# An output projection moved from feature-major tiles to a token-major group in seven products, with the embedding's projection moved in front of the MLP

## The chip, the cores and the metric

One core of one Trainium2 chip runs the whole program. The metric is the device time of one execution in microseconds (us); lower is better. An execution of the kernel before took 951.73 us in the median of three (951.28 to 951.88).

## What is computed

One layer of a decoder trunk on 512 tokens with 1024 features, all in 32-bit floats:

```python
mix = (sigmoid(gA) * (oA @ w_o_gla) + sigmoid(gB) * (oB @ w_o_attn)) @ w_out
x  += mix
x  += relu(RMSNorm(x) @ w_mlp1)^2 @ w_mlp2      # D_FF = 4096
x  += sigmoid(RMSNorm(x) @ w_pg) * (p @ w_pp)   # p: 512 x 256
out = RMSNorm(x)
```

The change touches the product with `w_out` (1024 x 1024), the residual x behind it, and the product `p @ w_pp` (256 x 1024).

## The kernel before, in words

*Products.* A 32-bit operand is kept as two parts in fp32r, a rounded "hi" and the rest "lo". A product takes three matmuls: hi by hi, hi by lo, lo by hi (`three`). ACT makes hi by a copy, DVE makes lo by a subtraction; this pair is called a split here. Weights come in pieces of 128 x 1024 (512 KB), about 250, through `fetch` (L306 to L325): while one operand is in use, DVE makes the lo of a later one (L297), ACT the hi of the next (L319), and a further one is loaded on SP's queue. All three happen in a fixed order in the engines' instruction streams, each of which is worked off strictly in order.

*Three forms of a projection.* `fm` is feature-major: the weight is the stationary operand, all 512 tokens stream, and a tile of 128 features takes 8 x 3 matmuls of 512 columns. `strassen` and `wide` use the scheme with seven products in place of eight of half the size: the weight quarters A11 to A22 and their sums S1 to S4 meet the activation quarters B11 to B22 and their sums T1 to T4. `strassen` is feature-major with 256 columns a matmul; `wide` is token-major: the activations are stationary, and the weight streams with 512 columns. A stage is one of the seven products: 24 matmuls. Stages share PSUM banks: a bank must be read (`begin`, a copy by ACT into SBUF) before a later stage accumulates into it, and `end` adds a bank to that copy. The order of stages in `wide`:

```python
WIDE = (("A11", "B11", "a"), ("S1", "T1", "c"), ("S2", "T2", "a"), ("A12", "B21", "b"), ("S3", "T3", "a"),
        ("S4", "B22", "c"), ("A22", "T4", "a"))
WBEGIN = {0: ((0, 0), "a"), 1: ((1, 1), "c"), 2: ((0, 1), "a")}
```

*Order of the work.* The program is written out by a generator. PE's stream is the frame; behind every few matmuls (`run`, in pieces) one deferred step of the list `later` is issued on the other engines, and one of the generators in `side`. So what an engine does, and when, follows from where a step was put on the list.

*Around the change.* `og` (the product with `w_o_gla`) makes 8 feature-major tiles; DVE multiplies each by its gate and adds it to the other branch (L1278, L1279), which gives the tiles of `mix`, split by `split_later` or, the last, by `split`. `wo` makes 8 feature-major tiles from them; each is added by DVE to the tile `xx[j]` of the transposed input (L1367, loaded by POOL at L1289). `x1_tile` scales each tile by the norm's weight (L1330) and makes the operands of `m1` (the first MLP projection, 8 groups `m1q0` to `m1q7` in `strassen`) with their sums and splits. During `m1q0`, `to_tokens` transposes the residual on PE (L1310, 32 transposes) and ACT copies it (L1314), since the second MLP projection adds token-major; `stats` sums the squares over the features with four one-column matmuls (L498).

*The embedding.* `pp0` and `pp1` (2 x 4 tiles of 128 tokens, 48 matmuls of 512 columns, `tmaj`) stand between the second MLP projection and `pg`, the last projection, which starts with tokens 0. ACT evacuates them (L1577). They lie beside the transposes (L1488) and splits of x3, the operand of `pg`.

Of the kernel before, what the change touches and what calls it, by code (L numbers as in the profile page):

```python
# [48 lines left out]
def weight_units():  # L49
# [39 lines left out]
    fm("wo", "w_out", 0, 8)  # L89
# [6 lines left out]
    for j in range(2):  # L96
        u.append((f"pp{j}.0", "tm", "w_pp", 0, j * 512))
# [79 lines left out]
NU, NW, PIECE, WAYS = 67, 5, 8, 2  # L177
# [6 lines left out]

NWARM = 9
# [3 lines left out]
def block_kernel(ctx, tc, xT, ws, pT, wts, wha, wa2, vec, lnf, rel, onehot, ident_d, mask_d, out):  # L189
    nc = tc.nc  # L190
    V, S, TE, SY, GP = nc.vector, nc.scalar, nc.tensor, nc.sync, nc.gpsimd

    const = ctx.enter_context(tc.tile_pool(name="const", bufs=1))
# [64 lines left out]
    def sums(i):  # L258
        q, _, what = OPERANDS[i].partition(".")
        if q.startswith("m2c"):  # L260
            if what[:3] == "S2.":
                w = raw[OPERANDS[i]] = raw[f"{q}.S1{what[2:]}"]
                V.tensor_tensor(w, w, raw[f"{q}.A11{what[2:]}"], op=OP.add)
            elif OPERANDS[i] in S4_LOADED:
                w = raw[OPERANDS[i]]
                V.tensor_tensor(w, w, raw[f"{q}.S2{what[2:]}"], op=OP.add)
        elif what[:3] in ("S2.", "S4."):
# [33 lines left out]
    def fetch(upto):  # L301

        while done[0] < min(upto, len(OPERANDS) - 1):
            i = done[0] = done[0] + 1
            if i >= 0:
# [6 lines left out]
                if q.startswith("m2c") and what[:2] == "S2" and f"{q}.S4{what[2:]}" not in S4_LOADED:  # L312
                    w = raw[f"{q}.S4{what[2:]}"] = raw[OPERANDS[i]]
                    GP.dma_start(w, wts[UNIT[f"{q}.A12{what[2:]}"]], accum_op=OP.add)
# [38 lines left out]
    def tmaj(name, n, lhs, evac, tts=range(4)):  # L353
# [3 lines left out]
        for tt in tts:  # L357
# [3 lines left out]
            if tt < 3:  # L361
                run(mms)
# [53 lines left out]
    def wide(name, xo, finish):  # L416


        bank, sums = {}, {}

        def begin(m, t, n, b):
            def go():
                sums[m, t, n] = u32()
# [6 lines left out]
        for i, (op, xname, b) in enumerate(WIDE):  # L430
# [76 lines left out]
    def rms_gen(acc, res, wait=0, gap=0, squared=False):  # L507
# [15 lines left out]
        bc = const.tile([P, T], F32, tag="rstd", name="rstd", bufs=2)  # L523
# [751 lines left out]
    mix = [None] * KC  # L1275
    for j in range(KC):
# [9 lines left out]
    xx = []  # L1286
    for j in range(KC):
        t = u32()
        GP.dma_start(t, xT[j * P:(j + 1) * P, :])  # L1289
        xx.append(t)  # L1290

    acc1, norm2 = [], []
    x2 = {}

    def stats():
        for _ in range(30):
            yield
        r = rms_tok(acc1[0], True)
        n = const.tile([P, 4], F32, name="nrm2")
# [3 lines left out]
    def to_tokens():  # L1303
        for m in range(2):
            for t in range(2):
                pts = [smt() for _ in range(2)]
                for n in range(2):
                    tok = slice((2 * t + n) * P, (2 * t + n + 1) * P)
                    for i in range(4):
                        TE.transpose(pts[n][:, i * P:(i + 1) * P], xx[4 * m + i][:, tok], ident)  # L1310
                yield
                for n in range(2):
                    x2[m, t, n] = u32()
                    S.activation(x2[m, t, n], pts[n], AF.Copy)  # L1314
                yield

    blk, xop = [None, None], {}
    def operand(name, g, x):
        xop[name, g] = split(x)

    def x1_tile(j):

        x, c = xx[j], cv[:, C_LN2 + j:C_LN2 + j + 1]
        g, p, k = j // 4, j % 4 // 2, j % 2

        def first():
            if blk[g] is None:
                blk[g] = [[u32(), u32()], [u32(), u32()]]
            for t in range(2):
                V.tensor_scalar(blk[g][k][t][:, halves(p)], x[:, halves(t)], c, None, op0=OP.mult)  # L1330
            sq = square(x)
            if j:
                V.tensor_tensor(acc1[0], acc1[0], sq, op=OP.add)
            else:
                acc1.append(sq)

        def left():
            (b11, b12), _ = blk[g]
            operand("B11", g, b11)
            t1 = u32()  # L1340
            V.tensor_tensor(t1, b11, b12, op=OP.subtract)
            operand("T1", g, t1)
            blk[g].append(t1)

        names, srcs, his = ("T4", "T2", "B21", "B22", "T3"), [], []

        def sums():
            (_, b12), (b21, b22), t1 = blk[g]
            t2, t3, t4 = u32(), u32(), u32()
            minus(t2, t1, b22)  # L1350
            minus(t4, t2, b21)
            his.append(split_hi(t4))
            V.tensor_tensor(t3, b22, b12, op=OP.subtract)
            srcs.extend((t4, t2, b21, b22, t3))

        def splits(i):
            def go():
                if i < 4:
                    his.append(split_hi(srcs[i + 1]))
                xop[names[i], g] = split_lo(srcs[i], his[i])  # L1360
            return go

        return [first] + {2: [left], 3: [sums] + [splits(i) for i in range(5)]}.get(j % 4, [])

    for j in range(KC):
        ps = fm(f"wo.{j}", mix)
        V.tensor_tensor(xx[j], xx[j], ps, op=OP.add)  # L1367
        later.extend(x1_tile(j))
    side.append(stats())
    side.append(to_tokens())  # L1370


    hid, hb, hx = [None] * 8, {}, {}
# [75 lines left out]
    pt, lnb = [], []  # L1449
# [48 lines left out]
    def last_inputs():  # L1498
        for k in range(2):
# [247 lines left out]
```

## Time and profile before

| | |
|---|---|
| median of three executions | 951.73 us |
| the profiled execution, its own time | 951.71 us |
| span in the profile | 949.6 us |
| PE busy (matmul) | 941.3 us, 99% |
| DVE busy | 726.5 us, 77% |
| ACT busy | 540.8 us, 57% |
| POOL busy | 102.9 us, 11% |
| chain that ended last | PE 98% |
| granted clock, mean | 0.998 |

Busy time is time in which an engine has an instruction at work; neighbours on one engine overlap, so the sum of single durations is longer. The chain is followed back from the last instruction, at each step to what released it. A duration in a row that ends in "x3" is that of three instructions together; where one starts is a better price than how long it lasts, since the next starts before it ends.

### The profile page before, as it was taken

How to read it: one execution, taken by the hardware profiler on the slowest of the kernel's cores; microseconds unless marked ns; L12 is line 12 of the kernel's file. 1: busy time of each engine (PE TensorE's matmuls, PEld its weight loads, DVE VectorE, ACT ScalarE, POOL GpSimd, SP SyncE). 2: the span in 40 equal slices, each digit the busy share in tenths (PEclk: the TensorE clock that was granted, in tenths of full speed). 3: DMA queues.
4: the chain of work that ended last, by engine and by line, in shares of the span. 5: the costliest groups of instructions: out<-in, count | busy, mean ns of one | idle time of the engine just before them, and what ended most of it. 6: DMA issues, size and time to landing. Idle time of an engine off the chain costs nothing.

```text
span 949.6 us, 15089 instructions
## 1 busy us (share of the span) xinstructions
PE 941.3 (99%) x5892; PEld 849.4 (89%) x5892; DVE 726.5 (77%) x1029; ACT 540.8 (57%) x880; POOL 102.9 (11%) x143
## 2 busy tenths in 40 slices
PE   9999999999999999999999999999999999999997
PEld 8789998899988888999988889999999888888886
DVE  7698879866789589878855788677777788988554
ACT  7357546445675479775732448555566445555643
POOL 0150010120100012022020000001000010020000
PEclk9999999999999999999999999999999999999999
DMA  9474482973818466456563436655647546796102
GB/s 352 142 236 114 129 201 68 289 234 100 200 46 227 159 144 182 132 134 200 156 199 92 131 89 173 154 142 134 162 129 191 141 100 166 218 306 222 53 0 89
DMA packets 46022, 150.34 MB, mean 158 GB/s; under 512 B 6723, under 2 KB 7311, under 8 KB 45952
## 3 DMA queue, kind: packets, MB, share of 16 engines
q1 hardware_dynamic: 29664, 100.61, 31.1%
q0 software_dynamic: 12608, 44.26, 23.5%
q10 hardware_dynamic: 3680, 4.51, 1.3%
q8 instruction: 46, 0.75, 0.3%
q14 instruction: 24, 0.20, 0.1%
HBM read 143.03 MB, written 8.17 MB: 159 GB/s over the span
## 4 chain that ended last, share of the span: by engine, by line
PE 98%; issue 1%; DMA 0%; ACT 0%; DVE 0%; POOLq 0%; POOL 0%; DVEq 0%
PE mmt L333 78%; PE smt L333 10%; PE mmt L581 2%; PE smt L1015 2%; PE smt L955 1%; PE smt L878 1%; PE smt L848 0%; PE smt L972 0%; PE smt L961 0%; PE smt L847 0%; PE smt L971 0%; PE smt L1310 0%; PE smt L1171 0%; PE smt L1071 0%; DMA cv<-in_vec_dram 0%
## 5 line engine op out<-in xcount | busy, mean ns | idle before, releaser
L333 PE MATMUL mmt<-ur,hi 128*128 128x256 f32 (+1 forms) x2320 | 476.0, 302 | 0.0
L333 PEld LDWEIGHTS mmt<-ur,hi 128*128 128x128 f32 x2320 | 373.1, 188 | 16.6
L333 PE MATMUL mmt<-ur,lo 128*128 128x256 f32 (+1 forms) x1160 | 351.2, 303 | 0.0
L297 DVE TENSOR_TENSOR lo<-w,hi 128x1024 fp32r<-128x1024 f32 x248 | 302.1, 1221 | 56.9 <-PE mmt L333 35.9
L319 ACT ACTIVATE hi<-w 128x1024 fp32r<-128x1024 f32 x248 | 259.2, 1054 | 93.8 <-PE mmt L333 24.5
L333 PE MATMUL mmt<-hi,ur 128*128 128x512 f32 (+3 forms) x832 | 241.1, 374 | 0.0
L333 PEld LDWEIGHTS mmt<-ur,lo 128*128 128x128 f32 x1160 | 218.6, 188 | 8.2
L333 PEld LDWEIGHTS mmt<-hi,ur 128*128 128x128 f32 x832 | 150.3, 188 | 25.7
L333 PE MATMUL mmt<-lo,ur 128*128 128x512 f32 (+3 forms) x416 | 154.8, 372 | 0.0
L461 ACT ACTIVATE ur<-u 128x512 fp32r<-128x512 f32 x111 | 66.1, 624 | 87.2 <-DVE u L1279 30.9
L333 PEld LDWEIGHTS mmt<-lo,ur 128*128 128x128 f32 x416 | 78.2, 188 | 13.6
L297 DVE TENSOR_TENSOR ur<-u,ur 128x512 fp32r<-128x512 f32 x110 | 72.7, 688 | 11.8 <-ACT ur L461 9.5
L333 PE MATMUL smt<-hi,ur 128*128 128x512 f32 x256 | 79.1, 390 | 0.0
L454 DVE TENSOR_TENSOR u<-u,mmt 128x512 f32<-128x512 f32 (+1 forms) x88 | 54.2, 647 | 26.9 <-PE mmt L333 26.6
L401 ACT ACTIVATE u<-mmt 128x512 f32<-128x512 f32 x72 | 43.1, 598 | 52.6 <-PE mmt L333 52.5
L250 POOL DMA_DIRECT2D w<-in_wts_dram x42 | 40.2, 1001 | 246.1 <-DMA w<-in_wts_dram 94.0
L333 PEld LDWEIGHTS smt<-hi,ur 128*128 128x128 f32 x256 | 47.8, 188 | 9.8
L276 POOL DMA_DIRECT2D w<-in_wts_dram x18 | 16.1, 894 | 317.9 <-DVE w L273 156.9
L333 PE MATMUL smt<-lo,ur 128*128 128x512 f32 x128 | 49.8, 389 | 0.0
L1389 ACT ACTIVATE u<-u 128x512 f32<-128x512 f32 x24 | 15.0, 628 | 26.7 <-DVE u L1385 26.7
L333 PEld LDWEIGHTS smt<-lo,ur 128*128 128x128 f32 x128 | 24.0, 188 | 5.0
L1250 ACT ACTIVATE u<-u 128x256 f32<-128x256 f32 x32 | 11.4, 411 | 20.9 <-DVE u L454 20.9
(235 smaller groups left out, 838.1 us busy)
## 6 DMA issues: line engine op xcount, KB each, us to landing
w<-in_wts_dram SPq DMA_DIRECT2D x180, 512.0 KB, 4.7
w<-in_wts_dram POOLq DMA_DIRECT2D x64, 512.0 KB, 6.8
u<-in_xT_dram SPq DMA_DIRECT2D x8, 256.0 KB, 5.3
u<-in_ws_dram SPq DMA_DIRECT2D x8, 256.0 KB, 5.4
v_dram<-u ACTq DMA_DIRECT2D x8, 256.0 KB, 6.6
u<-v_dram POOLq DMA_DIRECT2D x8, 256.0 KB, 6.2
y_dram<-u ACTq DMA_DIRECT2D x8, 256.0 KB, 2.0
u<-y_dram POOLq DMA_DIRECT2D x8, 256.0 KB, 6.2
```

The costliest lines, as they stand in the source:

```text
L250: GP.dma_start(w, wts[UNIT[b]], accum_op=OP.add)
L276: GP.dma_start(w, wts[UNIT[f"{q}.A21"]], accum_op=OP.add)
L297: V.tensor_tensor(lo, x, hi.bitcast(F32), op=OP.subtract)
L319: S.activation(hi[:, s], w[:, s], AF.Copy, scale=1.0 if c is None else c)
L333: TE.matmul(o, lhsT=l, rhs=r, start=a, stop=b, skip_group_check=shared)
L401: S.activation(sums[c], bank[b], AF.Copy, scale=-scale if c[0] else scale)
L454: V.tensor_tensor(out, s, ps, op=OP.subtract if m else OP.add)
L461: S.activation(hi, x, AF.Copy)
L581: TE.matmul(q0ps[i], lhsT=(hi, hi, lo)[j][:, c], rhs=(xh, xl, xh)[j], start=not k and not j, stop=k == KC - 1 and j == 2)
L1015: TE.matmul(o, lhsT=l[a][:, lc], rhs=r[b], start=start and i == 0, stop=stop and i == 2)
L1250: S.activation(outs[n], s[:, halves(n)], AF.Sigmoid)
L1389: S.activation(s, s, AF.Square)
```

## The change

1. `wo` becomes a token-major group in seven products (`quadw` weights, 14 operands in place of 8 tiles; `wide`). The sums of the weights are made as for the other groups, by DVE (L275 of the changed kernel) or by accumulating loads on POOL (L253, L319).
2. `mix_pair` makes the stationary operands of `wo` during `og`: per pair of tiles two 256-wide subtractions (L1299, L1300), two 256-wide sums (`minus`, L622), splits of both tiles (L474, L302), and for every second pair splits of the sums T1, T2, T4.
3. The residual x is loaded token-major on POOL. `begin` and `end` of `wo` add PSUM banks straight onto it on DVE (L467); a third copy isn't made. As each quarter is finished, `x1_ready` transposes it (L1380, 4 x 8 transposes), ACT copies it scaled (L1388), and sums and splits follow.
4. The sum of squares is taken token-major: eight `Square` with an accumulator on ACT (L1360), then three small DVE operations (L1363 to L1365) whose results scale m1's outputs. The one-column matmuls are gone.
5. `pp0` and `pp1` stand between `wo` and `m1`. ACT evacuates each tile (L1449) and issues its DMA to DRAM (L1450); eight POOL loads (L1588) bring them back during the second MLP projection.
6. `pg` takes tokens in the order 2, 3, 0, 1.

The core of the diff:

```diff
-    fm("wo", "w_out", 0, 8)
+    quadw("wo", "w_out", (0, 512))
+    for j in range(2):
+        u.append((f"pp{j}.0", "tm", "w_pp", 0, j * 512))
...
+TTS = (2, 3, 0, 1)
...
-    def wide(name, xo, finish):
+    def wide(name, xo, finish, base=None):
...
-        bank, sums = {}, {}
+        bank, sums = {}, dict(base or {})
         def begin(m, t, n, b):
             def go():
+                if base:
+                    return add(m, base[m, t, n], base[m, t, n], bank[b][n])
                 sums[m, t, n] = u32()
...
-                later.extend(end(m, t, n, b) for n in range(2))
+                ends = [end(m, t, n, b) for n in range(2)]
+                if base:
+                    later[0:0] = ends
+                else:
+                    later.extend(ends)
...
+    def mix_pair(pr):
+        e, f = tb[2 * pr], tb[2 * pr + 1]
+        g, o = pr // 2, halves(pr % 2)
+        t1, t2, t4 = (msums[name][g][:, o] for name in ("T1", "T2", "T4"))
+        his = {}
+        def sums():
+            V.tensor_tensor(t1, e[:, halves(0)], e[:, halves(1)], op=OP.subtract)
+            V.tensor_tensor(e[:, halves(1)], f[:, halves(1)], e[:, halves(1)], op=OP.subtract)
+            his["e"] = split_hi(e)
+        def second():
+            mix[2 * pr] = split_lo(e, his["e"])
+            minus(t2, t1, f[:, halves(1)])
+            minus(t4, t2, f[:, halves(0)])
+            if pr % 2:
+                his["T1"] = split_hi(msums["T1"][g])
...
     for j in range(KC):
         py = fm(f"og.{j}", og)
         V.tensor_tensor(ga[j], py, ga[j], op=OP.mult)
         V.tensor_tensor(tb[j], tb[j], ga[j], op=OP.add)
-        if j < KC - 1:
-            split_later(tb[j], mix, j)
-        else:
-            mix[j] = split(tb[j])
-    drain()
+        if j % 2:
+            later.extend(mix_pair(j // 2))
...
     def stats():
-        for _ in range(30):
-            yield
-        r = rms_tok(acc1[0], True)
+        ss = const.tile([P, 8], F32, name="ss1")
+        for (m, t, n), x in sorted(x2.items()):
+            sq, c = u32(), 4 * m + 2 * t + n
+            S.activation(sq, x, AF.Square, scale=1.0 / 32.0, accum_out=ss[:, c:c + 1])
+            yield
...
+    def evac_pp(j):
+        def go(tt, ps):
+            y = u32()
+            S.activation(y, ps, AF.Copy)
+            S.dma_start(pp_dram[4 * j + tt], y)
+        return go
+    later.extend(lambda k=k: pt.__setitem__(k, split(pt[k])) for k in range(2))
+    wide("wo", mix_op, onto_x, base=x2)
+    for j in range(2):
+        tmaj(f"pp{j}", 1, lambda k, tt: cols(pt[k], slice(tt * P, (tt + 1) * P)), evac_pp(j), piece=3)
```

*How it moves instructions.* The rows below give line, operation, output <- input by the program's names, the size, and how often it repeats. `u` are 32-bit tiles in SBUF, `ur` their fp32r parts, `w`, `hi`, `lo` a weight and its parts, `mmt` PSUM banks.

DVE at the end of `og` and the start of `wo`, before (L1278 and L1279 gate the last `og` tile):

```order
L297 TENSOR_TENSOR ur<-u,ur 128x512
L1278 TENSOR_TENSOR u<-mmt,u 128x512
L1279 TENSOR_TENSOR u<-u 128x512
L297 TENSOR_TENSOR ur<-u,ur 128x512
L297 TENSOR_TENSOR lo<-w,hi 128x1024
L1367 TENSOR_TENSOR u<-u,mmt 128x512
```

and in the changed kernel (L1338 and L1339 gate the last tile; L467 is the add onto x):

```order
L1338 TENSOR_TENSOR u<-mmt,u 128x512
L1339 TENSOR_TENSOR u<-u 128x512
L302 TENSOR_TENSOR lo<-w,hi 128x1024
L275 TENSOR_TENSOR w<-w 128x1024
L1299 TENSOR_TENSOR u<-u 128x256
L1300 TENSOR_TENSOR u<-u 128x256
L302 TENSOR_TENSOR ur<-u,ur 128x512
L622 SCALAR_TENSOR_TENSOR u<-u 128x256 x2
L302 TENSOR_TENSOR ur<-u,ur 128x512 x2
L302 TENSOR_TENSOR lo<-w,hi 128x1024
L275 TENSOR_TENSOR w<-w 128x1024
L302 TENSOR_TENSOR ur<-u,ur 128x512 x4
L302 TENSOR_TENSOR lo<-w,hi 128x1024
L467 TENSOR_TENSOR u<-u,mmt 128x512 x2
```

The last tile's split stood right behind its add; now a weight's lo, a weight sum and the two subtractions stand between them, and the adds of the first finished bank stand behind eleven further operations.

ACT in front of the first `begin` copy of `m1q0`, before (L461 and L319 make hi parts, L491 is a square, L401 the copy):

```order
L319 ACTIVATE hi<-w 128x1024
L491 ACTIVATE u<-u 128x512
L461 ACTIVATE ur<-u 128x512 x2
L319 ACTIVATE hi<-w 128x1024
L401 ACTIVATE u<-mmt 128x512
```

and in the changed kernel (L1449 and L1450 are the last evacuations of `pp1`, L1360 the squares, L408 the copy):

```order
L1449 ACTIVATE u<-mmt 128x512
L1450 DMA pp_dram<-u 128x512
L474 ACTIVATE ur<-u 128x512
L324 ACTIVATE hi<-w 128x1024
L1449 ACTIVATE u<-mmt 128x512
L1450 DMA pp_dram<-u 128x512
L474 ACTIVATE ur<-u 128x512
L1360 ACTIVATE u,ss_6165<-u 128x512
L474 ACTIVATE ur<-u 128x512
L1360 ACTIVATE u,ss_6165<-u 128x512 x2
L324 ACTIVATE hi<-w 128x1024
L408 ACTIVATE u<-mmt 128x512
```

The copy now stands behind the evacuations of the embedding with their DMA issues, three of the eight squares, and splits that stood earlier, beside `wo`.

## Rows read from the trace of the kernel before

**Rows 1.** The page: busy us of PE, the chain by engine, weight loads (busy, mean ns).

```profile
PE 941.3 (99%) x5892; PEld 849.4 (89%) x5892; DVE 726.5 (77%) x1029; ACT 540.8 (57%) x880; POOL 102.9 (11%) x143
...
PE 98%; issue 1%; DMA 0%; ACT 0%; DVE 0%; POOLq 0%; POOL 0%; DVEq 0%
...
L333 PEld LDWEIGHTS mmt<-hi,ur 128*128 128x128 f32 x832 | 150.3, 188 | 25.7
```

**Rows 2.** The waits of PE, whole span: total us, times, longest.

```profile
PE smt L553 <- POOL ones L548: 1.0, 1, 1.0
PE mmt L581 <- ACT ur L566: 0.3, 1, 0.3
```

**Rows 3.** Timeline of PE in the first group of m1: start, us, instruction, count.

```profile
562.91 0.40 PE L333 MATMUL mmt<-ur,hi 128*128 128x256 f32 x2
...
566.48 1.04 PE L1310 MATMUL smt<-ident,u 128*128 128x128 f32 x8
567.27 0.48 PE L333 MATMUL mmt<-ur,hi 128*128 128x256 f32 x2
...
601.38 0.95 PE L498 MATMUL smt<-ones,u 128*128 128x1 f32 x8
602.19 0.37 PE L333 MATMUL mmt<-ur,lo 128*128 128x256 f32 x1
```

**Rows 4.** Windows: og, wo, start of m1, end of the span; length, then busy.

```profile
472.83:516.35 43.52, 43.52 (x194) 36.04 (x193) 24.26 (x31) 13.38 (x19) 5.20 (x9) 1.00 0.50 155
516.35:559.88 43.53, 43.53 (x193) 36.04 (x192) 32.25 (x52) 17.17 (x24) 2.52 (x3) 1.00 0.31 88
559.88:580.00 20.12, 20.12 (x173) 20.11 (x172) 17.93 (x24) 16.47 (x28) 0.18 (x1) 1.00 0.61 156
946.00:949.50 3.50, 0.00 (x0) 0.00 (x0) 0.00 (x0) 0.00 (x0) 0.00 (x0) 0.56 0.41 150
```

The columns behind the length are busy us (instructions) of PE, PEld, DVE, ACT and POOL, then granted clock, DMA share and GB/s.

**Rows 5.** Timelines of DVE and ACT at the seam between og and wo.

```profile
516.56 0.69 DVE L1278 TENSOR_TENSOR u<-mmt,u 128x512 f32<-128x512 f32 x1 [2.29 <-PE mmt L333]
517.28 0.69 DVE L1279 TENSOR_TENSOR u<-u 128x512 f32<-128x512 f32 x1
...
518.01 0.63 ACT L461 ACTIVATE ur<-u 128x512 fp32r<-128x512 f32 x1 [4.81 <-DVE u L1279]
```

**Rows 6.** Timeline of DVE, queued back to back, at two places.

```profile
457.03 1.22 DVE L297 TENSOR_TENSOR lo<-w,hi 128x1024 fp32r<-128x1024 f32 x1
458.28 1.23 DVE L279 TENSOR_TENSOR w<-w 128x1024 f32<-128x1024 f32 x1
459.42 0.75 DVE L1163 TENSOR_TENSOR u<-u 128x256 f32<-128x256 f32 x2
...
545.66 1.89 DVE L297 TENSOR_TENSOR ur<-u,ur 128x512 fp32r<-128x512 f32 x3
```

**Rows 7.** Timeline of ACT: evacuation with DMA issue, hi, scaled copies, splits, square.

```profile
326.81 0.60 ACT L1221 ACTIVATE u<-mmt 128x512 f32<-128x512 f32 x1 [2.26 <-PE mmt L333]
...
327.81 1.06 ACT L319 ACTIVATE hi<-w 128x1024 fp32r<-128x1024 f32 x1 [0.40 <-ACT u L1221]
...
344.03 1.07 ACT L319 ACTIVATE hi<-w 128x1024 fp32r<-128x1024 f32 x1
344.98 0.85 ACT L1132 ACTIVATE u<-smt,grs 128x256 f32<-128x256 f32 x2
345.69 1.08 ACT L319 ACTIVATE hi<-w 128x1024 fp32r<-128x1024 f32 x1
...
544.66 1.66 ACT L461 ACTIVATE ur<-u 128x512 fp32r<-128x512 f32 x3
...
938.03 0.63 ACT L1610 ACTIVATE u<-u 128x512 f32<-128x512 f32 x1 [1.48 <-DVE u L1606]
938.57 0.19 ACT L1610 ACTIVATION_READ_ACCUMULATOR u<-u 128x1 f32 x1
```

**Rows 8.** Accumulating loads of L250 on POOL, from issue to landing.

```profile
DMA to landing us min/median/max: 5.3/7.9/13.2
```

More of the change, by code (lines that the diff above doesn't have):

```diff
@@ L266, in sums @@
                 V.tensor_tensor(w, w, raw[f"{q}.S2{what[2:]}"], op=OP.add)
+        elif q == "wo" and what[:3] == "S4.":
+            return
         elif what[:3] in ("S2.", "S4."):
@@ L360, in tmaj @@
                              for k in range(2 * n)])
-            if tt < 3:
-                run(mms)
+            if tt != last:
+                run(mms, piece)
             else:
@@ L1274, in block_kernel, with third, fourth, fifth @@
     pace[0] = 2048
-    mix = [None] * KC
+    mix, mx = [None] * KC, {}
+    msums = {name: [u32(), u32()] for name in ("T1", "T2", "T4")}
+    def mix_pair(pr):
[13 more added lines that the diff above has]
+                his["T1"] = split_hi(msums["T1"][g])
+        def third():
+            his["f"] = split_hi(f)
+            if pr % 2:
+                mx["T1", g] = split_lo(msums["T1"][g], his["T1"])
+        def fourth():
+            mix[2 * pr + 1] = split_lo(f, his["f"])
+            if pr % 2:
+                his["T2"] = split_hi(msums["T2"][g])
+        def fifth():
+            mx["T2", g] = split_lo(msums["T2"][g], his["T2"])
+            his["T4"] = split_hi(msums["T4"][g])
+        def sixth():
+            mx["T4", g] = split_lo(msums["T4"][g], his["T4"])
+        return [sums, second, third, fourth] + ([fifth, sixth] if pr % 2 else [])
+    def mix_op(name, pr):
+        if name in ("B11", "T3"):
+            return cols(mix[2 * pr], halves(int(name == "T3")))
+        if name in ("B21", "B22"):
+            return cols(mix[2 * pr + 1], halves(int(name == "B22")))
+        return cols(mx[name, pr // 2], halves(pr % 2))
     for j in range(KC):
@@ L1365, in block_kernel, with x1_parts, turn, copies @@
[L1365 to L1368, printed above, removed]
+    blk, xop = {}, {}
+    def x1_parts(m, t):
+        banks = []
+        def turn():
+            for k in range(2):
+                banks.append(smt())
+                for p in range(2):
+                    for n in range(2):
+                        i = 2 * p + k
+                        TE.transpose(banks[k][:, p * 256 + n * P:p * 256 + (n + 1) * P],
+                                     x2[m, t, n][:, i * P:(i + 1) * P], ident)
+        def copies(k):
+            def go():
+                blk[k, t, m] = u32()
+                for p in range(2):
+                    c = C_LN2 + 4 * m + 2 * p + k
+                    S.activation(blk[k, t, m][:, halves(p)], banks[k][:, halves(p)], AF.Copy, scale=cv[:, c:c + 1])
+            return go
+        return [turn, copies(0), copies(1)]
@@ L1562, in m2_seven @@
                 last_inputs()
-            elif (op, c) == ("A22", 2):
-                later.append(lambda: pt.__setitem__(slice(0, 2), [split(t) for t in pt]))
     pace[0] = 4608
@@ L1640, in evac_pg1 @@
         put(tt, slice(0, 512))
-    tmaj("pg0", 4, x3_op, evac_pg0)
-    tmaj("pg1", 4, x3_op, evac_pg1, tts=range(3))
+    tmaj("pg0", 4, x3_op, evac_pg0, TTS, 4)
+    drain()
+    tmaj("pg1", 4, x3_op, evac_pg1, TTS[:3], last=-1)
+    tt = TTS[-1]
     parts, sgs = [slice(0, LAST), slice(LAST, 512)], []
```

176 lines of the change are left out of this document (84 added, 92 removed).

## The prediction, made before the changed kernel was run

> **What bounds the kernel now.** I read the page's engine and chain parts first. TensorE (PE) is busy for 941.3 of the span's 949.6 us, and 98% of the chain that ended last is PE [rows 1]. The waits of PE come next: two, 1.0 and 0.3 us, both at the very start [rows 2]. So PE's instruction stream is the time. A matmul taken out of it is worth its full pitch, and anything that makes PE wait costs its full length, since now nothing makes it wait. The remaining views give prices: the pitch of PE's forms [rows 3], how full the other engines are around the change [rows 4], how the seam between `og` and `wo` runs now [rows 5], and what one operation costs DVE and ACT when they are queued back to back [rows 6, 7]. The profiled execution took 951.71 us, 0.02 below the median of 951.73, so a sum against it is a sum against the median. I count under 0.2% (1.9 us) as no change, which is about what a measurement of this kernel can tell.
>
> **What is removed.** `wo` is 192 matmuls of 512 columns in 43.53 us [rows 4], 0.2267 us each. Seven products of 24 are 168: 24 fewer, -24 x 0.2267 = **-5.44 us**. The Trainium skill (TensorE: Matmul & The Clock Gate, "Back-to-back issue gap") gives 518 cycles for 512 columns, which at 2.4 GHz would be an estimated 0.216 us, and 5.2 us here; the row is longer, so the row decides. The four one-column matmuls of L498 hold up the stream from 601.38 to 602.19 [rows 3], and their work goes to ACT and DVE: **-0.81**. The 32 transposes remain (L1380 for L1310). The 48 matmuls of `pp0`/`pp1` only move. Gain: **6.25 us**.
>
> **What is added: the seams.** Before, the 8th operand of `wo` was needed only at the 22nd matmul, so a late split was covered. Now both the operands and the results run through more DVE and ACT steps at points where PE soon needs them. I go along DVE's and ACT's queues in the order shown ahead.
>
> *Seam 1, og to wo.* PE ends `og` at 516.35. DVE multiplies at 516.56 and adds at 517.28 [rows 5]; a 512-wide operation lets the next start 0.61 us later (three splits in 1.89 [rows 6]), so DVE is free at 517.89. In its queue now stand a weight's lo (1.25) and a weight sum (1.14), then two 256-wide subtractions (0.75) [rows 6]: 521.03. Only then can ACT split the last pair (0.63 [rows 7]; a hand-over takes 0.04, as from 517.28 + 0.69 to 518.01 [rows 5]): 521.74. PE wants that operand at the 19th matmul, 516.35 + 18 x 0.2267 = 520.43: 1.31. Its lo ends 0.69 later on DVE, at 522.47, where the next matmul wants it at 521.97: 0.50. **+1.8.** If the two weight operations cost nothing it would be nothing (0 is the lower end), but DVE takes them in this order, after the add.
>
> *Seam 2, the third stage.* S2 accumulates into the bank that two adds onto x (`begin`, now on DVE) must have read first. From 521.74 DVE has: the lo split 0.61, two 256-wide sums 0.75 (priced as the pair of subtractions), two splits 1.21, lo 1.25, weight sum 1.14, four splits 2.42 (two of them of p, for the moved embedding), lo 1.14, add 0.69 (as 0.69 of a 512-wide operation [rows 5]) = 9.2: 530.95. PE is there at 516.35 + 48 x 0.2267 + 1.8 = 529.0. **+1.95.** Before, nothing read a bank of `wo` under such a condition. Without the embedding's two splits it would be 0.7.
>
> *Seam 3, transposes in wo.* They stand nine matmuls, 2.04 us, after a stage's end. Two adds after the stage's end alone take 0.21 + 0.61 + 0.69 = 1.5 and are covered. With a split and a weight's lo ahead they take 0.6 + 1.2 + 0.6 + 0.7 = 3.1, with lo alone up to 2.6. The order has them behind lo for two of the three groups: 1.05 and 0.5. **+1.5** (0 to 2).
>
> *Seam 4, S2 of the first group of m1.* The begin copy is now the last of a long ACT queue. ACT gets the first `pp` result when PE ends it. From there to the copy's end: 8 evacuations with a DMA issued by ACT at 1.00 (326.81 to 327.81), 9 splits at 0.54 (1.66 for three, the last runs 0.63), 4 weight hi at 0.95 (344.03 to 344.98), 4 scaled copies at 0.36 (two take until 345.69), 3 squares at 0.63 (0.54 to the accumulator read, then about half of its 0.19), the copy 0.60 [rows 7]: 8.00 + 4.86 + 3.80 + 1.44 + 1.89 + 0.60 = 20.6. PE meanwhile has 42 matmuls of 512 (9.52), 8 transposes (566.48 to 567.27: 0.79), and 72 of 256 at 0.119 (30 from 562.91 to 566.48) [rows 3], 8.55: 18.9. **+1.75.** With an accumulator read in full it is 2.0. ACT already holds 16.5 of 20.1 us there now, DVE 17.9 [rows 4].
>
> *Seam 5, behind the statistics.* The three small DVE operations wait for all eight squares, and a weight's lo stands behind them. From the copy's end: 5 squares 3.15, hi 0.95, copy 0.5, then on DVE about 0.5 and lo 1.22 = 6.4 with hand-overs. PE reaches that lo after 50 matmuls of 256, 5.95. **+0.45.**
>
> Sum of the waits: 1.8 + 1.95 + 1.5 + 1.75 + 0.45 = **7.45**. After a wait on the stationary operand its load is no longer hidden: one takes 188 ns [rows 1]. Eight to nine waits at 0 to 0.19 each give 0 to 1.6; I take the middle, **+0.8**.
>
> **Costed at nothing.** x and p are loaded on POOL's queue long before use, like the xT loads they replace, and eight read-backs of 256 KB take the place of two loads of p, hundreds of us ahead; the write to DRAM is of the eight DMAs' issue time only, counted in seam 4. The embedding stood before the last projection as 48 matmuls, 10.9 us, of cover for the transposes and splits of x3. That cover is gone; in its place tokens 2 and 3 go first, with 48 matmuls on operands that are ready. If that cover failed, up to two splits of x3 with their transposes, about 2 us, would show. The tail has the same operations in another token order. The sums and splits made during `og` find DVE busy for 24.3 of 43.5 us and ACT for 13.4 [rows 4].
>
> **Sum:** 951.71 - 6.25 + 7.45 + 0.8 = 953.7. The waits are differences of queues of 9 and 20 us: a 5% error in the DVE or the ACT pitch moves seam 2 or 4 by 0.5 to 1.0 each, so about 1.5 us either way together. The forecast is **953.7 us**, and 952.2 to 956 its own range.
>
> **Rivals.**
> 1. *Not slower: the queues drain faster than summed.* Seams 1 to 3 hang on one DVE queue (5 us long at seam 1, 9.2 at seam 2) and seams 4 and 5 on one ACT queue (20.6 and 6.4 us). If neighbours on an engine overlap more than in the rows I priced them by, every seam shrinks by that share of its queue: at 5% by 0.25 + 0.45 + 0.15 + 1.0 + 0.3 = 2.15 us, which is 951.6, no change; at 10% twice that, 949.4, faster. It decides as soon as it is there at all, since the forecast stands 0.1 us above the bound of no change. For it: some forms stand in mixed rows here that no row shows in this mix. Against it: I took pitches, not durations, and the seam before, worked out in this way, meets its own rows within 0.1 us (517.28 + 0.69 + 0.04 = 518.01 [rows 5]).
> 2. *The waits vanish:* only the 6.25 us remain, 945.5. For it: the other projections in seven products run without one wait of PE [rows 2]. Against: seam 1 and 2 follow from the order of one engine with rows of this trace.
> 3. *A weight comes late.* One half of S3's weight is accumulated by a POOL DMA that stands behind another, which waits for a DVE lo of S2. By my times it may take about 8.2 us to land; accumulating loads of L250 take 7.9 in the median and 13.2 at most [rows 8]. At the worst 5 us more: 957 to 959.
> 4. *The clock falls at the waits.* The rows show 1.00 through all of the stretches with work and 0.56, near the lower of the two levels (1.2 of 2.4 GHz), only where PE did nothing for 3.5 us [rows 4]. My longest wait is 2 us. How long the clock would stay down no row shows; if as long as each wait, half of 7.45 us is lost on top: 957.4. The Trainium skill (TensorE: Matmul & The Clock Gate, "A second HAM failure mode: psum-queue depth-cycling") tells of short pauses between groups of matmuls that let the clock swing. No row here shows that; by that rule this rival would be the forecast.
>
> **Chances.** The seams as summed (952.2 to 956) 0.55, of which 0.25 lie within 0.2% (below 953.6) and 0.30 above; rival 1 (949.4 to 952.2) 0.22, of which 0.05 is faster by over 0.2%; rival 2 0.07; rival 3 0.11; rival 4 0.05. Faster: 0.05 + 0.07 = 0.12. Same: 0.25 + 0.17 = 0.42. Slower: 0.30 + 0.11 + 0.05 = 0.46. The range from 949.6 to 957.5 holds the first case, nearly all of rival 1 and a third of the last two, 0.8.
>
> **What would show it.** Right: PE's list of waits, empty now, names DVE and ACT: about 1.8 us at the first pair of products on the last operand pair, 2 us at the start of S2 for the adds, about 0.5 each at the transposes for the adds, 1.7 us at m1's S2 for the copy; the last `pp` evacuations and the squares back to back on ACT. Wrong: no wait of PE between `og` and m1 (rival 2); a wait on a `w` loaded by POOL, or on hi behind it (rival 3); a granted clock below 1.00 after 516 (rival 4); a wait of PE in `pg0` (the cover I costed at nothing); or matmuls of 512 with another pitch than 0.2267.

## The result, and the profile after

The changed kernel took 954.73 us in the median of seven executions (953.24 to 955.35), the kernel before 951.88 beside it: a ratio of 1.0025, with a 95% interval of 1.0013 to 1.0037. It is slower by a quarter of a per cent, although PE does less. The profiled execution, with 955.35 us, is the longest of the seven.

The page of the changed kernel, where the rows on busy time and on the chain answer to [rows 1]:

```profile
span 953.6 us, 15140 instructions
...
PE 938.1 (98%) x5860; PEld 844.3 (89%) x5860; DVE 741.4 (78%) x1042; ACT 552.1 (58%) x908; POOL 111.3 (12%) x157
...
PE 94%; ACT 2%; DVE 2%; issue 1%; ACTq 0%; POOL 0%; POOLq 0%; DVEq 0%
```

PE is busy 3.2 us less and the span is 4.0 us longer. Before, PE was 98% of the chain; now ACT and DVE stand on it with 2% each. The list of PE's waits (us in total, times, longest) had two rows at the start of the program [rows 2]; five new ones have come, and they name the two engines:

```profile
PE smt L1380 <- DVE u L467: 2.6, 5, 1.5
PE mmt L338 <- DVE u L467: 1.8, 1, 1.8
PE mmt L338 <- ACT u L408: 1.4, 1, 1.4
PE mmt L338 <- ACT ur L474: 1.3, 1, 1.3
PE smt L566 <- POOL ones L561: 1.0, 1, 1.0
PE mmt L338 <- DVE ur L302: 0.2, 1, 0.2
```

The timeline of PE says where they lie (start, length, instruction, and in brackets how long PE stood idle and for whom):

```profile
521.78 0.50 PE L338 MATMUL mmt<-hi,ur 128*128 128x512 f32 x1 [1.28 <-ACT ur L474]
522.51 0.50 PE L338 MATMUL mmt<-hi,ur 128*128 128x512 f32 x1 [0.23 <-DVE ur L302]
...
531.13 0.70 PE L338 MATMUL mmt<-hi,ur 128*128 128x512 f32 x2 [1.76 <-DVE u L467]
...
545.84 0.33 PE L1380 MATMUL smt<-ident,u 128*128 128x128 f32 x1 [1.50 <-DVE u L467]
...
586.90 0.50 PE L338 MATMUL mmt<-ur,hi 128*128 128x256 f32 x2 [1.38 <-ACT u L408]
```

These are seams 1, 1, 2, 3 and 4 of the forecast. The fourth row, at 545.84, stands at the first transposes, where the forecast had no wait. DVE at seams 1 and 2, to be read beside [rows 5, 6]:

```profile
517.18 0.69 DVE L1339 TENSOR_TENSOR u<-u 128x512 f32<-128x512 f32 x1
517.79 1.22 DVE L302 TENSOR_TENSOR lo<-w,hi 128x1024 fp32r<-128x1024 f32 x1
519.04 1.23 DVE L275 TENSOR_TENSOR w<-w 128x1024 f32<-128x1024 f32 x1
520.19 0.42 DVE L1299 TENSOR_TENSOR u<-u 128x256 f32<-128x256 f32 x1
520.64 0.42 DVE L1300 TENSOR_TENSOR u<-u 128x256 f32<-128x256 f32 x1
521.76 0.69 DVE L302 TENSOR_TENSOR ur<-u,ur 128x512 fp32r<-128x512 f32 x1 [0.70 <-ACT ur L474]
...
526.77 2.49 DVE L302 TENSOR_TENSOR ur<-u,ur 128x512 fp32r<-128x512 f32 x4
529.17 1.22 DVE L302 TENSOR_TENSOR lo<-w,hi 128x1024 fp32r<-128x1024 f32 x1
530.31 1.28 DVE L467 TENSOR_TENSOR u<-u,mmt 128x512 f32<-128x512 f32 x2
```

The first split starts at 521.76 (summed: 521.74 plus a hand-over), and the first add ends near 531.0 (summed: 530.95). And what stands behind the wait of 1.5 us, on ACT and DVE:

```profile
541.73 2.01 ACT L324 ACTIVATE hi<-w 128x1024 fp32r<-128x1024 f32 x2 [10.89 <-PE smt L338]
545.53 1.06 ACT L324 ACTIVATE hi<-w 128x1024 fp32r<-128x1024 f32 x1 [1.79 <-DMA w<-in_wts_dram]
```

```profile
542.83 2.36 DVE L302 TENSOR_TENSOR lo<-w,hi 128x1024 fp32r<-128x1024 f32 x2 [4.30 <-ACT hi L324]
545.10 1.28 DVE L467 TENSOR_TENSOR u<-u,smt 128x512 f32<-128x512 f32 x2
```

DVE stood idle for 4.3 us, then did the lo of two late weights, and only then the two adds that the transposes need. The weight behind the first row is the accumulated half of S3 from the forecast's third rival. Issued at 531.49, it took, by the answer for that one DMA (min, median and max are the same):

```profile
DMA to landing us min/median/max: 10.1/10.1/10.1
```

It landed at 541.63, 0.1 us before ACT's first row starts (that row names a releaser on PE; e2 below tells which of the two it was). A window of that time shows what it stood beside; the columns are those of [rows 4], with the DMA engines fully busy where the whole of `wo` had 0.31 of them before:

```profile
538.00:540.00 2.00, 2.00 (x10) 1.65 (x10) 0.52 (x1) 0.00 (x0) 0.00 (x0) 1.00 1.04 272
```

### The profile page after: what moved, and what is told of

Same layout as the page of the kernel before. It is cut to its first block, busy times and chain, and to the rows that moved or that the text cites. A ratio compares the mean times of both kernels' runs of the same rounds, so it can differ in the third digit from the quotient of the medians.

```text
span 953.6 us, 15140 instructions
## 1 busy us (share of the span) xinstructions
PE 938.1 (98%) x5860; PEld 844.3 (89%) x5860; DVE 741.4 (78%) x1042; ACT 552.1 (58%) x908; POOL 111.3 (12%) x157
## 4 chain that ended last, share of the span: by engine, by line
PE 94%; ACT 2%; DVE 2%; issue 1%; ACTq 0%; POOL 0%; POOLq 0%; DVEq 0%
PE mmt L338 73%; PE smt L338 11%; PE mmt L594 2%; PE smt L1028 2%; PE smt L968 1%; PE smt L891 1%; DVE lo L302 1%; ACT hi L324 1%; ACT u L1360 1%; PE smt L566 0%; DVE u L467 0%; PE smt L861 0%; PE smt L985 0%; PE smt L984 0%; PE smt L860 0%
## 5 line engine op out<-in xcount | busy, mean ns | idle before, releaser
L338 PE MATMUL mmt<-ur,hi 128*128 128x256 f32 (+1 forms) x2192 | 436.5, 298 | 1.4 <-ACT u L408 1.4
L338 PEld LDWEIGHTS mmt<-ur,hi 128*128 128x128 f32 x2192 | 347.9, 188 | 13.3 <-ACT u L408 1.6
L302 DVE TENSOR_TENSOR lo<-w,hi 128x1024 fp32r<-128x1024 f32 x254 | 308.6, 1220 | 58.5 <-PE mmt L338 35.1
L338 PE MATMUL mmt<-ur,lo 128*128 128x256 f32 (+1 forms) x1096 | 324.9, 296 | 0.1
L338 PE MATMUL mmt<-hi,ur 128*128 128x512 f32 (+3 forms) x928 | 271.6, 376 | 3.3 <-DVE u L467 1.8
L338 PEld LDWEIGHTS mmt<-ur,lo 128*128 128x128 f32 x1096 | 207.0, 189 | 5.9 <-DVE lo L302 0.3
L338 PEld LDWEIGHTS mmt<-hi,ur 128*128 128x128 f32 x928 | 168.1, 188 | 33.5 <-ACT hi L324 2.2
L338 PE MATMUL mmt<-lo,ur 128*128 128x512 f32 (+3 forms) x464 | 173.6, 374 | 0.0
L474 ACT ACTIVATE ur<-u 128x512 fp32r<-128x512 f32 x117 | 69.4, 625 | 80.0 <-DVE u L1300 31.1
L338 PEld LDWEIGHTS mmt<-lo,ur 128*128 128x128 f32 x464 | 87.2, 188 | 15.4
L302 DVE TENSOR_TENSOR ur<-u,ur 128x512 fp32r<-128x512 f32 x116 | 76.5, 687 | 19.2 <-ACT ur L474 18.7
L467 DVE TENSOR_TENSOR u<-u,mmt 128x512 f32<-128x512 f32 (+1 forms) x100 | 61.9, 653 | 27.0 <-PE mmt L338 26.7
L408 ACT ACTIVATE u<-mmt 128x512 f32<-128x512 f32 x72 | 42.8, 595 | 50.0 <-PE mmt L338 49.8
L253 POOL DMA_DIRECT2D w<-in_wts_dram x46 | 44.3, 1012 | 221.1 <-DMA w<-in_wts_dram 127.1
L844 ACT ACTIVATE u<-u,st 128x256 f32<-128x256 f32 (+1 forms) x32 | 15.6, 489 | 12.5 <-DVE st L840 11.0
```

What stands on the lines that cost most here:

```text
L253: GP.dma_start(w, wts[UNIT[b]], accum_op=OP.add)
L302: V.tensor_tensor(lo, x, hi.bitcast(F32), op=OP.subtract)
L338: TE.matmul(o, lhsT=l, rhs=r, start=a, stop=b, skip_group_check=shared)
L408: S.activation(sums[c], bank[b], AF.Copy, scale=-scale if c[0] else scale)
L467: V.tensor_tensor(out, s, ps, op=OP.subtract if m else OP.add)
L474: S.activation(hi, x, AF.Copy)
```

## The experiments

The pitch of the 256-column matmuls of m1 turned out to have two values; the profiles show which by the number of matmuls between 605 and 705 us (835 or 836 is 120.0 ns, 845 is 118.7 ns), and the table gives it. Over m1 the difference is 1.5 us. Each run left one profile, so the column holds for one execution of each. "Waits" is what PE's stream lost between 470 and 600 us, from start to start, above its pitch, by steps of 0.15 us and more. Matmuls at half the granted clock count in it: 1.4 us of the 6.5 in e3 and 1.6 of the 11.1 in e7. The kernel before was run beside each set, with medians of 951.88 to 952.04.

| run | edit | median us | ratio to before (95%) | waits | 605 to 705 |
|---|---|---|---|---|---|
| before | | 951.9 | | 0 | 836 |
| changed | | 954.73 | 1.0025 (1.0013 to 1.0037) | 9.2 | 836 |
| e1_pool_issue | POOL issues the parking DMAs | 952.94 | 1.0011 (1.0002 to 1.0020) | 6.4 | 835 |
| e2_early_sum | S3 sums earlier | 951.56 | 1.0000 (0.9991 to 1.0009) | 7.0 | 845 |
| e3_p_late | splits of p later | 951.07 | 0.9992 (0.9983 to 1.0001) | 6.5 | 845 |
| e4_weight_early | first S1 lo earlier | 951.09 | 0.9993 (0.9984 to 1.0001) | 6.5 | 845 |
| e5_four_edits | all four | 946.01 | 0.9940 (0.9927 to 0.9952) | 0.4 | 835 |
| e6_split_first | last pair ahead of the weight | 953.09 | 1.0015 (1.0005 to 1.0024) | 8.4 | 845 |
| e7_embedding_back | embedding at its old place | 956.85 | 1.0057 (1.0042 to 1.0072) | 11.1 | 845 |
| e8_squares_alone | before, with the new statistics | 950.69 | 0.9989 (0.9980 to 0.9998) | 0 | 836 |
| e9_act_issue | e5 without e1's edit | 947.26 | 0.9951 (0.9938 to 0.9963) | 2.7 | 845 |
| e10_short_wait | e5 with a wait put in | 945.11 | 0.9930 (0.9917 to 0.9942) | 1.0 | 845 |
| e11_short_wait_before | before with that wait | 952.28 | 1.0004 (0.9995 to 1.0013) | 0.6 | 836 |

### One cause at a time

e1, the queue of ACT:

```diff
-            S.dma_start(pp_dram[4 * j + tt], y)
+            GP.dma_start(pp_dram[4 * j + tt], y)
```

> One edit to the changed kernel: the eight DMAs of the evacuated embedding tiles are issued by POOL instead of ACT. Theory: the wait at the second stage pair of m1's first group is ACT's queue; each issue keeps ACT from its next instruction for 0.40 us, eight for 3.2, against a wait of 1.4 us on the copy and 0.2 on the weight's lo behind the statistics. Both waits vanish, some 2.0 us with the reloads; the waits between og and the embedding stay. Time about 2 us below the changed kernel, 952.5 to 953. Rival: the queue is not the cause, or POOL's issues delay the accumulating loads for m1: the wait stays or moves to a weight, and the time stays near 954.7.

1.8 us less in the median, at the upper end of what was expected, and 3.0 in the profiled executions. In the list of PE's waits no row on the copy L408 is left, and PE doesn't wait for the weight's lo behind the statistics. In the changed kernel ACT reached the copy so (the third row's bracket is the time of the issue):

```profile
581.45 0.58 ACT L1449 ACTIVATE u<-mmt 128x512 f32<-128x512 f32 x1
582.06 0.33 ACTq L1450 DMA_DIRECT2D pp_dram<-u  x1
582.43 0.63 ACT L474 ACTIVATE ur<-u 128x512 fp32r<-128x512 f32 x1 [0.40 <-ACT u L1449]
...
586.28 0.57 ACT L408 ACTIVATE u<-mmt 128x512 f32<-128x512 f32 x1
```

and with POOL issuing, 3.9 us earlier, of which the execution was ahead by 0.8 us already:

```profile
582.39 0.58 ACT L408 ACTIVATE u<-mmt 128x512 f32<-128x512 f32 x1
```

The theory holds for seams 4 and 5. (The first transposes also waited 1.1 us less here, without an edit to them: the weight took 9.05 us instead of 10.1.)

e2, the late weight. The unit of the key is a weight in the order of use:

```diff
-        elif what[:3] == "S3." and q.startswith("m2c"):
+        elif what[:3] == "S3." and (q == "wo" or q.startswith("m2c")):
             EARLY.setdefault(i - 3, []).append((n, f"{q}.A11.{what[3:]}", f"{q}.A21.{what[3:]}"))
```

> One edit to the changed kernel: the accumulating loads for the two S3 weights of the output projection are made one weight earlier, so that on POOL's queue they stand before the two for S4, which wait for DVE. Theory: the longest wait in the profile, 1.5 + 0.5 us at the first transposes, stands behind a weight that landed 10.1 us after its issue at 531.49 (12.4 and 15.7 for the next two), in a stretch in which the DMA engines are fully busy (532 to 548); issued some 3 to 5 us earlier, before the burst, it lands in 6 to 8 us and the first transposes wait for nothing: 2.2 us less than the profiled changed kernel, 1.5 less in the median, and the runs lie closer together. Rival: the burst itself sets the landing, since the same bytes are to be moved at the same time: the wait stays, or is found at the S4 weights, and the time stays within 0.5 us of the changed kernel.

The first of the two loads now is issued at 498.37, 33 us earlier (3 to 5 were expected), since it no longer stands on POOL behind the load that waits for DVE, and takes

```profile
DMA to landing us min/median/max: 6.4/6.4/6.4
```

The first transposes wait for nothing; 2.2 us of waits are gone, and no other came. Of the five waits on L467 in that row of the changed kernel's list (2.6 us in all) three are left, at the two later groups:

```profile
PE smt L1380 <- DVE u L467: 0.8, 3, 0.3
```

That is what the theory said of the wait. On the size in the median (3.2 us less instead of 1.5) it was wrong. In the profile m1 ran at the other pitch, which fits the difference; that it did so in the other executions isn't shown.

e3, DVE's queue ahead of the third stage:

```diff
-    later.extend(lambda k=k: pt.__setitem__(k, split(pt[k])) for k in range(2))
-    wide("wo", mix_op, onto_x, base=x2)
+    rest = [lambda k=k: pt.__setitem__(k, split(pt[k])) for k in range(2)]
+    wide("wo", mix_op, onto_x, base=x2, rest=rest)
```

`wide` puts `rest` on the list behind the first two adds.

> One edit to the changed kernel: the two splits of p for the embedding stand behind the first two adds onto x, not ahead of them. Theory: the wait before the third stage is the length of DVE's queue; two splits are 1.21 us of it, so that wait falls from 1.8 to 0.6 us and the time by 1.2. Rival: the queue is not what sets it (the weight's hi or lo for the third stage ends as late): the wait stays and the time too.

The wait before the third stage is gone altogether, not down to 0.6, and the trace shows that this isn't DVE's doing alone. In this execution the granted clock fell behind the two waits of seam 1 (windows and timeline of e3):

```profile
523.60:526.60 3.00, 3.00 (x8) 2.34 (x7) 2.97 (x4) 1.28 (x2) 0.00 (x0) 0.50 0.00 0
```

```profile
523.65 0.63 PE L338 MATMUL mmt<-lo,ur 128*128 128x512 f32 x1
524.08 1.06 PE L338 MATMUL mmt<-hi,ur 128*128 128x512 f32 x2
524.93 0.63 PE L338 MATMUL mmt<-lo,ur 128*128 128x512 f32 x1
```

Seven matmuls ran at 0.426 us, 0.2 more than the pitch: PE came 1.4 us late to the third stage and so had no wait of 0.6 left to take. That the queue is 1.2 us shorter is shown; what it is worth at an unbroken clock this run doesn't show (e4 and e5 together do, below). The median fell by 3.7 us against 1.2 expected. What the profile shows beside the queue is the late weight (issued 1.25 us earlier, it landed in 8.3 us and the first transposes didn't wait) and the other pitch of m1.

e4, DVE's idle time before the last og tile:

```diff
         py = fm(f"og.{j}", og)
+        if j == KC - 1:
+            fetch(OPERAND["wo.S1.0"])
```

> One edit to the changed kernel: the lo of the first S1 weight and the weight sum behind it are issued one tile of og earlier, so that DVE does them in the 2.28 us in which it stands idle for PE before the last og tile. Theory: this takes 2.4 us out of the queue between the last gate and the first split: the waits of 1.3 and 0.2 us (with reloads 2.0) at the last operand pair vanish, the one before the third stage stays near 1.5, so 2 to 2.5 us less than the changed kernel. Rival: the wait only moves: DVE's work between og's end and the third stage is the same, so what is won at the first wait is lost at the second, and the time stays within 0.5 us.

The two waits of seam 1 are gone, and the third stage keeps 1.46 of 1.76 us:

```profile
529.77 0.70 PE L338 MATMUL mmt<-hi,ur 128*128 128x512 f32 x2 [1.46 <-DVE u L467]
```

The waits fell by 2.7 us, against 2 to 2.5 expected; the median fell by 3.6, and m1 ran at the other pitch in the profile (845). The rival, that the wait would only move, is out for this edit, which uses time in which DVE did nothing.

e6 asks the same question without that idle time: only the order is changed, so that the last pair goes first.

```diff
         if j % 2:
-            later.extend(mix_pair(j // 2))
+            steps = mix_pair(j // 2)
+            if j == KC - 1:
+                steps.pop(0)()
+                steps.pop(0)()
+            later.extend(steps)
```

> One edit to the changed kernel: at the last og tile the two subtractions, the first lo and the two sums of the last pair stand right behind the gate, ahead of the weight's lo and the weight sum. No DVE work is taken out of the stretch. Theory: DVE is the limit from og's end to the third stage, so the waits of 1.3 and 0.2 us at the last operand pair vanish, but a wait of some 1.9 us comes up at the lo of the second S1 weight, and the 1.8 us before the third stage stay: the time within 0.5 us of the changed kernel in the same state of the m1 stretch. Rival: the order alone was at fault: 2 us less, as in the run in which DVE's idle time was used.

```profile
526.68 0.50 PE L338 MATMUL mmt<-lo,ur 128*128 128x512 f32 x1 [1.77 <-DVE lo L302]
...
530.97 0.70 PE L338 MATMUL mmt<-hi,ur 128*128 128x512 f32 x2 [1.72 <-ACT hi L324]
```

Seam 1 is gone, and a wait of the same length stands at the lo of the second S1 weight, with the third stage as late as before. The row of that stage names a hi of ACT, and this had itself waited for DVE's weight sum L275:

```profile
527.98 3.90 ACT L324 ACTIVATE hi<-w 128x1024 fp32r<-128x1024 f32 x4 [2.71 <-DVE w L275]
```

From 470 to 532 us PE loses 3.8 us here and 3.9 in the changed kernel. The theory holds: between og's end and the third stage the sum of DVE's work is the limit, and another order of it doesn't help. The median is 1.6 us lower; the profile has two things for it, the pitch of m1 (845) and the first transposes (1.3 instead of 2.2).

### All parts together, and parts alone

e5 is the changed kernel with the edits of e1, e2 and e4, and the splits of p put behind the first finished quarter of x instead of behind the first adds:

```diff
+            if (m, t) == (0, 0):
+                later.extend(lambda k=k: pt.__setitem__(k, split(pt[k])) for k in range(2))
```

> The changed kernel with all four parts: POOL issues the embedding's DMAs, the S3 sums one weight earlier, the splits of p behind the first finished quarter of x, and the first S1 weight's lo one og tile earlier. Theory: the waits are queues of DVE and ACT and one late weight, and nothing else stands behind them; what is left is one wait of some 0.3 us before the third stage, so the full gain of 6.25 us shows but for 0.3 to 0.6: 951.9 - 5.8 = 946.1, or 1.5 less where the 256-column stretch of m1 runs at the pitch of 118.7 ns in place of 120.0. Rival: the waits move on to a stage that now has slack (the weights' lo, the DMA burst): 948 to 950.

946.01 us, against 946.1 expected, 0.6% below the kernel before. The page and the one new wait:

```profile
PE 935.7 (99%) x5860; PEld 844.2 (89%) x5860; DVE 741.3 (79%) x1042; ACT 552.1 (58%) x908; POOL 115.6 (12%) x165
```

```profile
PE mmt L338 <- ACT hi L324: 0.3, 1, 0.3
```

```profile
527.38 0.70 PE L338 MATMUL mmt<-hi,ur 128*128 128x512 f32 x2 [0.26 <-ACT hi L324]
```

This is the third stage. Ahead of it e5 and e4 have the same DVE queue but for the two splits of p, which cost 1.21 us as summed, and the clock is 1.00 in both. From start to start the wait is 0.42 us in e5 and 1.62 in e4, so the splits cost what the queue said; what is left waits for a hi and no longer for the adds.

The busy times of DVE and ACT are those of the changed kernel to 0.1 us. The same work, at other places in the queues, took 8.7 us less.

e7 undoes one part of the change, the place of the embedding (`pp` units, evacuation, p's loads and the token order as before; `flush()` behind `wide("wo", ...)`, since no `pp` matmuls are left to issue the steps beside).

> The changed kernel with one part undone: the embedding's 48 matmuls stand between the second MLP projection and the last one again, with tokens in the old order and nothing parked in DRAM; all steps of x's last quarters are issued at the end of the output projection. Theory: the embedding is the cover for the adds, transposes, copies and splits behind the last stage; without it PE waits for the last two adds (some 2 us), for the first split of the second half (some 3) and for a lo behind them (1.5), some 6.5 us, while the waits on the m1 copy and behind the statistics (2.0 with reloads) and half of the one before the third stage (1.2) go: 2 to 4 us slower than the changed kernel, 956.5 to 959. Rival: the move is what costs (eight evacuations with DMAs on ACT, two splits on DVE): undoing it gives 2 to 3 us back, near 952.

956.85 us, 2.1 above the changed kernel, although its m1 ran at the faster pitch; waits of 11.1 us. Behind the end of `wo` PE now waits at the places that were expected, for the last adds and for the first splits of the second half, 5.2 us in all from start to start where 6.5 were expected:

```profile
564.73 0.30 PE L1375 MATMUL smt<-ident,u 128*128 128x128 f32 x1 [1.49 <-DVE u L467]
...
569.68 0.38 PE L338 MATMUL mmt<-ur,hi 128*128 128x256 f32 x1 [2.04 <-ACT ur L474]
570.49 0.58 PE L338 MATMUL mmt<-ur,hi 128*128 128x256 f32 x1 [0.42 <-DVE ur L302]
```

So the embedding in front of the MLP covers those steps in the changed kernel. With the four edits of e5 its place was not tried. The clock fell twice in this profile as well, behind the waits of seam 1 and behind these; one of the two windows:

```profile
570.50:573.80 3.30, 3.30 (x15) 3.30 (x16) 3.20 (x6) 1.81 (x4) 0.00 (x0) 0.50 0.00 0
```

e8 is another part alone, on the kernel before:

```diff
-        r = rms_tok(acc1[0], True)
+        for (m, t, n), x in sorted(x2.items()):
+            sq, c = u32(), 4 * m + 2 * t + n
+            S.activation(sq, x, AF.Square, scale=1.0 / 32.0, accum_out=ss[:, c:c + 1])
...
-            sq = square(x)
-            if j:
-                V.tensor_tensor(acc1[0], acc1[0], sq, op=OP.add)
```

> The kernel before with one part of the change alone: the sum of squares is taken by eight squares with an accumulator on the token-major residual, and the four one-column matmuls, the eight feature-major squares and their seven adds are gone. Theory: 0.81 us of PE's stream go and nothing waits: 951.1. Beside it the trace of the kernel before shows the pitch of the 256-column matmuls going from 118.9 to 120.0 ns right behind those one-column matmuls, and staying there for 130 us. If they set it, it stays at 118.7 to 118.9 and 1.3 to 1.5 us more are gained: 949.6. Rival: nothing is gained, since the squares on ACT make something late: 951.9.

1.35 us less in the median, 0.9 at PE's last matmul, no waits. The 0.81 are there. The pitch stayed at 120.0 from 605 us on, and already from 580 to 595 us e8 has 127 matmuls where the kernel before has 129, so the one-column matmuls alone don't set it.

### The two pitches of m1

e9 is e5 with ACT issuing again, that is, e2, e4 and the late splits of p.

> Three of the four edits (ACT issues the embedding's DMAs again). Theory: ACT's queue comes back as waits of some 2 us at the m1 copy and behind the statistics, and up to 1.2 at the splits of p, which now stand late: 2 to 3.2 us more than with four edits. But in every profile so far in which PE waited for that copy, the 256-column stream behind it ran at 118.7 ns (in one of them until a second, shorter wait), and in every one without a wait there at 120.0; if the wait decides it, 1.5 us come back over the next 130 us: 946.5 to 947.7. Rival: the pitch is chance, 948 to 949.2 in about half of the executions.

PE waits for the copy again:

```profile
PE mmt L338 <- ACT u L408: 0.8, 1, 0.8
```

It loses 2.7 us in all, 2.3 more than in e5, and the median is only 1.25 longer. m1 runs at 118.7 in the profile, which would give 1.5 back.

e10 adds a wait to e5; e11 adds the same to the kernel before:

```diff
+        if q == 1:
+            a, d, b = smt(), u32(), smt()
+            TE.transpose(a[:, 0:P], ident, ident)
+            V.tensor_scalar(d[:, 0:P], a[:, 0:P], 0.0, None, op0=OP.max)
+            TE.transpose(b[:, 0:P], d[:, 0:P], ident)
         strassen(f"m1q{q}", x1_op, finish, extra=first_splits(0) if q == 7 else None)
```

> The kernel with four edits, plus a wait put in on purpose: in front of m1's second group PE transposes the identity into a bank, DVE copies it, PE transposes the copy; nothing reads it. PE waits for DVE, some 0.6 to 1.5 us. Theory: a wait in the 256-column stream sets its pitch, which goes from 120.0 to 118.7 ns behind it and gives back 1.4 us over 120 us: 945.5 to 946.5, the same as without it. Rival: the pitch does not hang on a wait: 0.8 to 1.7 us slower, 946.8 to 947.7.

> The kernel before with the same wait put in ahead of m1's second group, where DVE's queue is shorter: PE waits some 0.4 to 0.8 us. The one-column matmuls of the statistics follow about 18 us later. Theory: the pitch goes to 118.7 ns behind the wait; if nothing sets it back, 1.4 us are won against 0.6 to 1.0 lost: 951.3, and if the one-column matmuls set it back to 120.0, 952.7. Rival: no change of pitch before or after them: 952.7, and the trace tells which.

With two transposes and a wait of 0.4 us more, the median is 945.11 where that of e5 is 946.01, a little below the range expected. The two were measured in different sets and their intervals overlap, so the gain in time is likely and not shown. The change of pitch stands in the profile of e10 itself: 120.0 up to the wait at 590 us and 118.7 from 592 us on. Windows from 605 to 705 us, of e5 and then of e10:

```profile
605.00:705.00 100.00, 100.00 (x835) 100.00 (x835) 73.06 (x85) 57.66 (x79) 7.89 (x9) 1.00 0.59 153
```

```profile
605.00:705.00 100.00, 100.00 (x845) 100.00 (x845) 73.96 (x86) 57.61 (x79) 7.87 (x9) 1.00 0.57 153
```

In the kernel before it is worth nothing: m1 was at 118.7 before the wait as well, went to 120.0 behind the one-column matmuls at 601 us, and the median rose by 0.4 us, about the wait and the transposes. Windows of e11, ahead of those matmuls and behind them (129 matmuls in 15 us against 127; a window counts those that reach into it, too):

```profile
585.00:600.00 15.00, 15.00 (x129) 15.00 (x128) 10.39 (x14) 7.74 (x14) 0.00 (x0) 1.00 0.70 199
603.00:618.00 15.00, 15.00 (x127) 15.00 (x127) 10.87 (x15) 9.66 (x16) 1.64 (x2) 1.00 0.80 198
```

## Why the prediction was right

The forecast was 953.7, slower, in a range of 949.6 to 957.5; it came to 954.73. The direction was right with a small margin: its own chances were 0.46 for slower and 0.42 for no change. Step by step, waits counted from start to start in the profile of 955.35:

- **Gain, 6.25.** e5 bears it out: with 0.4 us of waits left, its median lies 6.0 below the kernel before.
- **Seam 1, 1.8.** Measured 1.95. e4 and e6 show the cause.
- **Seam 2, 1.95.** Measured 1.92. The sum over a queue of thirteen operations came within 0.05 us. That DVE's queue sets it, e4 and e5 show: two splits less, 1.2 us less.
- **Seam 3, 1.5.** Measured 3.6: this is the term that was mis-sized. The second and third groups cost 0.94 and 0.49, as summed (1.05 and 0.5). The step that failed is "two adds after the stage's end alone take 1.5 and are covered", for the first group: its adds stood behind the lo of two weights that came late, 2.16 us. The mechanism was in the text, as the third rival, with its place, but as a case of its own at 5 us, not as a part of the sum. e2 took that wait out.
- **Seam 4, 1.75.** Measured 1.55; e1 took it out. **Seam 5, 0.45.** Measured 0.21.
- **Restarts, 0.8.** Some 0.6: the first matmul behind a wait was followed 0.06 to 0.11 us later than its pitch, against a middle of 0.09 in the forecast.
- Sum: 951.71 - 6.25 + 9.2 + 0.6 = 955.3, for 955.35. That it closes so well is in part luck: m1 ran at the same pitch in both profiles (836), and at the other it would have been 1.5 less.
- **Costed at nothing.** No wait of PE stands behind 593 us; the last projection is covered.

Rival 1 (shorter queues) is out: the waits of seams 1 and 2 are as long as summed, and those of seams 4 and 5 shorter by 0.2 us each, while seam 3 is longer. Rival 2 describes e5, after four edits, and not the changed kernel. Rival 4 isn't in the profile of the changed kernel: the granted clock is 1.00 from 472 to 700 us in it. But e3 and e7 show it behind the same waits of seam 1, at 0.50 for some 3 us, with 1.4 and 1.6 us lost; two of the seven executions of the changed kernel have a mean clock of 0.993 where the others have 0.997 or 0.998. The rule of the Trainium skill (TensorE: Matmul & The Clock Gate, "A second HAM failure mode: psum-queue depth-cycling"), that short pauses between groups of matmuls let the clock swing if they are frequent enough, agrees with e3 and e7 and not with the changed kernel's profile. As a forecast for this change, at the 957.4 of the rival, it would have been too slow.

What the forecast had no term for is the pitch of m1. The spread of the seven executions, 953.24 to 955.35, is as wide as the difference of the two pitches (1.5 us) with the late weight and the clock beside it; which execution had what can't be told, since only one of them has a trace.

## What to carry to other kernels

When PE's stream is the time, removed matmuls are paid at the places where other engines now have to be ready: go along the strictly ordered queue of each, from the last instruction that PE released to the one that PE needs, and add pitches; that sum was good to 0.25 us at four of five places, and missed the one where a weight came late. Moving work inside a stretch that is too full only moves the wait; moving it to where the engine stood idle, to another engine's queue, or behind the needed instruction took out all but 0.4 of 9.2 us. An accumulating load that stands behind one that waits for another engine starts late, and then meets every transfer that was held up with it: issue such loads by when they can start, not by when they are used.

## What the runs showed of the hardware that was not expected

- **Two pitches of one stream.** The 256-column matmuls with a weight load each run at 118.7 or at 120.0 ns, for 130 us on end. At 120.0 the steps between their starts repeat every three matmuls (117, 120 and 123 ns in the kernel before); at 118.7 every five (122, 120, 119, 115 and 118 in e10). In seven of the nine profiles in which PE waited in m1 ahead of 605 us (e2, e3, e4, e6, e7, e9, e10) it ran at 118.7 from 605 us on. In the four in which it did not wait there (before, e1, e5, e8) it ran at 120.0. The two exceptions are the changed kernel, which was at 118.6 behind its first wait and at 120.0 behind its second, and e11, which went to 120.0 right behind the one-column matmuls. A wait isn't needed for the faster pitch: the kernel before ran at 118.7 from 562 to 598 us without one. What decides it is open; in e10 it changed right behind the added wait of 0.4 us.
- **The clock.** A granted clock of 0.50 for some 3 us followed two waits of 1.4 and 0.5 us in e3 and e7, and not the same two waits in the changed kernel, e1 and e2, where it stayed at 1.00.
- **A DMA issue on ACT** kept ACT from its next instruction for 0.40 us in each of eight cases in the changed kernel.
- **Accumulating loads.** The same 512 KB took 6.4 us at a DMA share of 0.80 (e2, 498.4 to 504.7 us) and 10.1 us at a share of 0.95 (the changed kernel, 531.5 to 541.6 us).
